# Block products of an MLP in another order, their left sums on VectorE and their first weight sums by adding transfers

## The chip, the cores and the metric

The kernel runs on one core of a Trainium2 chip. A core has five engines with a queue each: TensorE (PE) multiplies, VectorE (DVE) and ScalarE (ACT) do elementwise work, GpSimd (POOL) does elementwise work and issues transfers, and SyncE (SP) issues transfers. Each engine takes its instructions in order, and an instruction that waits holds up all that stand behind it in its queue. The metric is the device time of one execution in microseconds (us). The time before is the median of 3 runs, 786.85 us (786.6 to 787.11).

## The reference, cut to what matters

The program is one layer of a transformer in fp32 over 512 tokens of width 1024: a gated linear attention and a latent attention side by side, an output projection, and an MLP of width 4096 with a squared ReLU. The change lies in the MLP and in the turn from the output projection into it:

```python
    merged = jax.nn.sigmoid(z_ma) * y_gla + jax.nn.sigmoid(z_mb) * y_mla
    h = h + merged @ w_out[l]
    m = rmsnorm(h, g_mlp[l])
    h = h + jnp.square(jax.nn.relu(m @ w_ff1[l])) @ w_ff2[l]
return rmsnorm(h, g_final)
```

## The kernel before

**Three matmuls for one.** Each fp32 operand is split into a high part, rounded to the matmul's format (a copy on ScalarE), and a low part, the rest (a subtraction on VectorE). `mm3` (lines 87 to 90) multiplies high by high, high by low and low by high. In the profile a split's two halves are named by their tile: `f150h` and `f150l` are the high and low of the weights of phase f1, product 5, half 0.

**Seven products for eight.** The large multiplications are cut into 2 x 2 blocks, and each is done with seven block products in place of eight, for which sums of blocks are formed on either side. For the weights (the right side), with blocks B11, B12, B21, B22: product 1 takes B11, product 2 takes B21, product 5 takes B11+B12, product 6 adds B22 to that, product 4 adds B21 to that, product 3 takes B22, product 7 takes B12+B22. The sums are formed in place, in the tiles into which the blocks were loaded. So product 5's weights can be formed only after product 1's have been split. For the left side the sums are 5 = A21-A22, 6 = sum 5 - A11, 7 = A11-A21, 3 = A12 + sum 6 (the signs are the code's).

**Phases.** The hidden width of 4096 is worked through in four quarters. Each has two phases: in phase f (f0 to f3) the normed rows are multiplied by a block of `w_ff1`, in phase g (g0 to g3) its result by a block of `w_ff2`. A product of an f phase is 48 matmuls of 256 columns, a product of a g phase 24 of 512. The class `Mlp` (lines 1543 to 1682) writes a phase, the loop behind line 1859 runs through all 56 products. At each step it first calls `prepare` for the product two steps ahead: B22 is added for product 6 on VectorE (`add`, line 1577), the weights are split in two halves of 128 x 1024 (`split_right`, ACT line 1582 and DVE line 1586), and `behind` issues what may follow. There are four buffers of highs and four of lows, which is two products' worth: a product's split can begin only when the product two before it is through.

**What `behind` does, before.** After product 1's split GpSimd adds B12 to B11 (line 1577), and a transfer issued by GpSimd adds B22 from memory onto B12 (`onto`, line 1572, `accum_op`). After product 6's split such a transfer adds B21 onto B11. After 2, 3, 7 and 4 SyncE loads the blocks of the phases to come (`load`, line 1568).

**The left side in a quarter.** `keep` takes the results of an f phase's products from the accumulators into the blocks A11, A12, A21, A22 of the hidden layer, with ReLU and square, and splits those that are finished (`split_left`, through `split`, lines 93 and 94). After product 4, the last of an f phase, `left_sums` forms sum 5 on VectorE and the sums 7, 6 and 3 on GpSimd (line 1664). Their splits follow in the g phase, at its first three products. In g each product's result is added to the rows `hrow` (`add_rows`, line 1465).

**The turn into the MLP.** From the output projection on (line 1745) up to the fourth product of f0 the order of TensorE, ScalarE and VectorE is written out: `in_program_order` ties each instruction to the one before it on its engine; the same holds for GpSimd over a longer stretch. In it, rows 0 and 1 are scaled (`row_rstd` has one power on GpSimd, line 184; `scaled` is lines 1479 and 1480), transposed on TensorE (`flipped`, line 198), and turned into the left blocks of f0 with the gain: `m_upper` for rows 0 to 255 splits straight from the accumulator, `m_upper_raw` forms the unsplit blocks again on GpSimd (line 1510), `m_lower` and `m_lower_raw` do rows 256 to 511, `m_sum` forms sums (line 1539), on GpSimd unless told otherwise. Behind that stretch the order of each engine is the framework's, which goes by the program's order and by what is ready.

Of the kernel before, what the change touches and what calls it, by code (L numbers as in the profile page):

```python
# [56 lines left out]
def tile_block(ctx: ExitStack, tc: tile.TileContext, t, out: bass.AP):  # L57
# [1436 lines left out]
    def m_upper():  # L1494

        for m in (1, 2):
            m_left[m] = quarter(f"mh{m}"), quarter(f"ml{m}")
        for k in range(KD):
            hi, lo = m_left[1 + k // NP]
            src, gain = fm.block(0, k)  # L1500
            split_scaled(hi[:, k % NP], lo[:, k % NP], src, gain)

    def m_upper_raw():

        for m in (1, 2):
            hi, lo = m_left[m]
            m_raw[m] = pair_tiles(f"mr{m}")
            for b, dst in enumerate(m_raw[m]):
                c = slice(2 * b, 2 * b + 2)
                nc.gpsimd.tensor_tensor(dst, raw(hi[:, c]), raw(lo[:, c]), op=ALU.add)  # L1510

    def m_split(m):
        m_left[m] = hi, lo = quarter(f"mh{m}"), quarter(f"ml{m}")
        for b, s in enumerate(m_raw[m]):
            c = slice(2 * b, 2 * b + 2)
            split(hi[:, c], lo[:, c], s)

    def m_lower():

        a22, s1 = pair_tiles("mr4"), pair_tiles("mr5")  # L1520
        m_raw[4], m_raw[5] = a22, s1
        for b in range(2):
            for i in range(2):
                src, gain = fm.block(1, NP + 2 * b + i)
                nc.scalar.activation(a22[b][:, i], src, AF.Copy, scale=gain)
                src, gain = fm.block(1, 2 * b + i)
                nc.vector.scalar_tensor_tensor(s1[b][:, i], src, gain, a22[b][:, i], op0=ALU.mult, op1=ALU.subtract)
        m_split(5)

    def m_lower_raw():  # L1530
        m_raw[0] = a21 = pair_tiles("mr0")
        for k in range(NP):
            src, gain = fm.block(1, k)
            nc.scalar.activation(a21[k // 2][:, k % 2], src, AF.Copy, scale=gain)

    def m_sum(m, x, y, op, eng=nc.gpsimd):
        m_raw[m] = pair_tiles(f"mr{m}")
        for dst, a, b in zip(m_raw[m], m_raw[x], m_raw[y]):
            eng.tensor_tensor(dst, a, b, op=op)
# [4 lines left out]
    class Mlp:  # L1544


        def __init__(self, n):
            self.n, self.qd, self.second = n, n // 2, n % 2 == 1
            self.name = f"{'g' if self.second else 'f'}{self.qd}"
            self.order = ORDER if n == 2 * NQ - 1 else SEVEN  # L1550
# [19 lines left out]
        def onto(self, dst, x):  # L1570
            for g, d in enumerate(self.tiles(dst)):
                nc.gpsimd.dma_start(d, self.source(x, g), accum_op=ALU.add)  # L1572

        def add(self, dst, x, eng, gs=range(2)):
            for g in gs:
                a, b = self.tiles(dst)[g], self.tiles(x)[g]
                eng.tensor_tensor(a, a, b, op=ALU.add)  # L1577
# [12 lines left out]
        def behind(self, m):  # L1590

            after_ = phases[self.n + 1 : self.n + 3]
            if m == 1:
                self.add(B11, B12, nc.gpsimd)
                self.onto(B12, B22)
            elif m == 6:
                self.onto(B11, B21)
            elif m == 4:
                if len(after_) == 2:
                    after_[1].load(B11)  # L1600
            elif m in (2, 3, 7) and after_:
                after_[0].load({2: B21, 3: B22, 7: B12}[m])

        def prepare(self, m):
            if m == 6:
                self.add(B11, B22, nc.vector)
# [24 lines left out]
        def keep(self, m):  # L1631
# [16 lines left out]
            if m in (2, 3, 7):  # L1648
                self.split_left(c)

# [7 lines left out]
        def left_sums(self):  # L1658

            a11, a12, a21, a22 = (self.left[x] for x in (1, 2, 0, 4))  # L1660

            def sums(eng, dst, a, b, op):
                for d, x, y in zip(dst, a, b):
                    eng.tensor_tensor(d, x, y, op=op)  # L1664

            sums(nc.vector, a22, a21, a22, ALU.subtract)
# [264 lines left out]
```

## Time and profile before

| | us |
|---|---|
| median of 3 runs | 786.85 |
| profiled execution, its own time | 788.59 |
| its span (first to last instruction) | 786.6 |
| TensorE busy | 746.1 |
| VectorE busy | 664.6 |
| ScalarE busy | 496.3 |
| GpSimd busy | 309.3 |

The profile is of one execution. Its views are a page with each engine's busy time; a table of busy time by stretch; a list of who waited for whom; and instructions in order of time. A row in order of time has its start, its length, engine, line, operation, output<-inputs with shapes, a count if like instructions follow one another, and in brackets the idle time before it with what ended it. `x2` after a row means that the length covers two instructions. "Granted clock" is the share of TensorE's full clock: 1.00 or, in some stretches, 0.50.

### The profile page before, as it was taken

To read this page: it belongs to the slowest core of one execution; us is meant where nothing else is said; L and a number is where in the kernel's file an instruction comes from. 1 tells how busy PE (TensorE), PEld (TensorE's weight loads), DVE (VectorE), ACT (ScalarE), POOL (GpSimd) and SP (SyncE) were. 2 spreads that over 40 slices of the span, in tenths; PEclk is the share of its full clock that TensorE was granted. 3 is DMA by queue.
4 is the path that set the end of the run, shared out by engine and by line. 5 is a ranking of instruction groups with operands and counts; after the bars stand their busy time and mean duration, and the time that the engine had idled before them with its cause. 6 is when DMAs were issued, how large, how long until landed. Compare 5 with 4: busy or idle time off the path is not lost.

```text
span 786.6 us, 11492 instructions
## 1 busy us (share of the span) xinstructions
PE 746.1 (95%) x4226; PEld 650.0 (83%) x4226; DVE 664.6 (84%) x830; ACT 496.3 (63%) x807; POOL 309.3 (39%) x323
## 2 busy tenths in 40 slices
PE   9999999999999999999998698899889997999796
PEld 7888888888988988989888696799768995799575
DVE  7786887899987877988989889885998789886994
ACT  7456665768667759888565684547544674367454
POOL 0722110265457241367518326140823145140934
PEclk9999999999999999999999899999989999999898
DMA  9759580612122244587964354757546743765332
GB/s 319 229 143 255 141 202 17 108 29 67 47 74 21 72 104 120 128 226 230 204 197 107 56 162 105 212 109 195 127 87 171 174 131 80 215 150 146 53 54 107
DMA packets 78343, 105.75 MB, mean 134 GB/s; under 512 B 15792, under 2 KB 34224, under 8 KB 78288
## 3 DMA queue, kind: packets, MB, share of 16 engines
q1 hardware_dynamic: 63088, 75.64, 30.9%
q0 software_dynamic: 14912, 29.10, 21.8%
q8 instruction: 33, 0.54, 0.3%
q10 hardware_dynamic: 288, 0.28, 0.1%
q14 instruction: 22, 0.18, 0.1%
HBM read 100.03 MB, written 2.10 MB: 130 GB/s over the span
## 4 chain that ended last, share of the span: by engine, by line
PE 72%; DVE 18%; issue 6%; ACT 3%; POOL 1%; DVEq 0%; POOLq 0%; ACTq 0%
PE first L326 3%; DVE h L1465 2%; PE tp L1122 2%; DVE w L1577 2%; PE zb L88 1%; PE zb L90 1%; PE zb L89 1%; DVE f0l L94 1%; DVE f1l L94 1%; DVE f2l L94 1%; PE av L89 1%; PE av L88 1%; PE av L90 1%; DVE f3l L94 1%; PE s L88 1%
## 5 line engine op out<-in xcount | busy, mean ns | idle before, releaser
L1577 POOL TENSOR_TENSOR w<-w,w 128x1024 f32<-128x1024 f32 x15 | 41.9, 2793 | 131.2 <-DVE g010l L1586 22.3
L1572 POOL DMA_DIRECT2D w<-in_w_ff x32 | 38.8, 1224 | 59.1 <-DVE f260l L1586 10.1
L1102 DVE TENSOR_REDUCE top<-s 128x1 f32<-128x512 f32 x32 | 21.6, 682 | 4.9 <-PE s L90 4.7
L1107 ACT ACTIVATE e<-s,top 128x512 f32<-128x512 f32 x32 | 22.0, 688 | 3.5 <-DVE top L1102 2.5
L94 DVE TENSOR_TENSOR pT<-tp,pT 128x512 fp32r<-128x512 f32 x32 | 21.8, 683 | 2.4 <-ACT pT L93 1.9
L94 POOL TENSOR_TENSOR qF<-qk,qF 128x512 fp32r<-128x512 f32 x4 | 6.6, 1640 | 37.6 <-ACT qF L93 37.6
L93 ACT ACTIVATE pT<-tp 128x512 fp32r<-128x512 f32 x32 | 19.1, 596 | 3.2 <-PE tp L1122 3.2
L94 DVE TENSOR_TENSOR f2l<-f2a,f2h 128x512 fp32r<-128x512 f32 x14 | 17.7, 1276 | 3.0 <-ACT f2h L93 2.8
L94 DVE TENSOR_TENSOR f1l<-f1a,f1h 128x512 fp32r<-128x512 f32 x14 | 17.7, 1276 | 3.0 <-ACT f1h L93 2.8
L667 POOL DMA_DIRECT2D gvw<-in_w_in x4 | 4.8, 1226 | 38.7 <-DVE gvw L672 34.0
L94 DVE TENSOR_TENSOR f3l<-f3a,f3h 128x512 fp32r<-128x512 f32 x14 | 17.1, 1230 | 2.8 <-ACT f3h L93 2.8
L1122 PE MATMUL tp<-ident,e 128*128 128x128 f32 x128 | 19.4, 274 | 0.0
L88 PE MATMUL av<-pT,v 128*128 128x256 f32 x64 | 19.1, 299 | 0.0
L90 PE MATMUL av<-pT,v 128*128 128x256 f32 x64 | 18.2, 284 | 0.0
L89 PE MATMUL av<-pT,v 128*128 128x256 f32 x64 | 18.1, 283 | 0.0
L1122 PEld LDWEIGHTS tp<-ident,e 128*128 128x128 f32 x128 | 15.2, 140 | 3.2 <-ACT e L1113 0.7
L667 POOL DMA_DIRECT2D zaw<-in_w_in x4 | 4.8, 1215 | 32.7 <-DVE zaw L672 28.0
L94 DVE TENSOR_TENSOR f0l<-f0a,f0h 128x512 fp32r<-128x512 f32 x14 | 13.1, 950 | 3.7 <-ACT f0h L93 3.7
L1153 POOL TENSOR_TENSOR mx<-tb,yg 128x256 f32<-128x256 f32 x8 | 7.7, 967 | 19.8 <-DVE tb L1150 13.8
L980 POOL DMA_DIRECT2D w<-in_w_out x10 | 12.3, 1402 | 6.5 <-DVE bo60l L94 5.3
L93 ACT ACTIVATE f0h<-f0a 128x512 fp32r<-128x512 f32 x14 | 8.5, 620 | 9.2 <-POOL f0a L1664 6.8
L88 PE MATMUL s<-kbuf,q 96*128 96x512 f32 x32 | 14.1, 439 | 0.0
(2143 smaller groups left out, 3360.6 us busy)
## 6 DMA issues: line engine op xcount, KB each, us to landing
w<-in_w_ff SPq DMA_DIRECT2D x48, 512.0 KB, 4.9
w<-in_w_ff POOLq DMA_DIRECT2D x32, 512.0 KB, 6.1
w<-in_w_out POOLq DMA_DIRECT2D x10, 512.0 KB, 8.6
grw<-in_w_in SPq DMA_DIRECT2D x8, 512.0 KB, 8.6
zaw<-in_w_in SPq DMA_DIRECT2D x8, 512.0 KB, 7.0
gvw<-in_w_in SPq DMA_DIRECT2D x8, 512.0 KB, 4.5
w<-in_w_out SPq DMA_DIRECT2D x16, 256.0 KB, 5.5
w220f<-in_w_ff SPq DMA_DIRECT2D x8, 512.0 KB, 6.4
```

The costliest lines, as they stand in the source:

```text
L88: nc.tensor.matmul(acc, lh, rh, start=start, stop=False, skip_group_check=onto)
L89: nc.tensor.matmul(acc, lh, rl, start=False, stop=False, skip_group_check=onto)
L90: nc.tensor.matmul(acc, ll, rh, start=False, stop=stop, skip_group_check=onto)
L93: nc.scalar.activation(hi, src, AF.Copy)
L94: rest.tensor_tensor(lo, src, raw(hi), op=ALU.subtract)
L326: nc.tensor.matmul(f_accs[i], a[:, i * P : (i + 1) * P], b, start=k == 0 and x == 0, stop=k == KD - 1 and x == 2)
L1102: nc.vector.tensor_reduce(top, acc, axis=AX.X, op=ALU.max, negate=True)
L1107: nc.scalar.activation(e, acc, AF.Exp, bias=top, accum_out=tot[:, qt % 2 : qt % 2 + 1])
L1122: nc.tensor.transpose(tp[:, k * P : (k + 1) * P], e[:, k * P : (k + 1) * P], ident)
L1465: nc.vector.tensor_tensor(hc, hc, acc, op=op)
L1572: nc.gpsimd.dma_start(d, self.source(x, g), accum_op=ALU.add)
L1577: eng.tensor_tensor(a, a, b, op=ALU.add)
```

## The change

- The order of the products is 1, 5, 6, 7, 2, 4, 3 in place of 1, 2, 5, 6, 3, 7, 4; in f0 it is 1, 2, 5, 6, 7, 4, 3. The last phase keeps its own order 1, 5, 6, 3, 7, 4, 2.
- B11+B12 is formed by a transfer that adds B12 from memory onto B11, right behind product 1's split. B12+B22 is formed by such a transfer one phase earlier, as soon as B12 has been loaded.
- All left sums are on VectorE. Sums 5, 7 and 6 and the splits of 5, 6 and 7 stand behind product 4, sum 3 and its split behind product 3.
- At the turn into the MLP the blocks are first copied out of the accumulators with the gain and then split, so that nothing has to be formed again; the sums are on VectorE and stand next to the products that need them.

```diff
+    def m_copy(x, half, ks):
+        ...
+            nc.scalar.activation(m_raw[x][p // 2][:, p % 2], src, AF.Copy, scale=gain)
+    def m_sum(m, x, y, op, bs=range(2)):
+        ...
+            nc.vector.tensor_tensor(m_raw[m][b], m_raw[x][b], m_raw[y][b], op=op)
...
-            self.order = ORDER if n == 2 * NQ - 1 else SEVEN
+            self.order = {0: (1, 2, 5, 6, 7, 4, 3), 2 * NQ - 1: ORDER}.get(n, (1, 5, 6, 7, 2, 4, 3))
...
+        def onto(self, dst, x, gs=range(2)):
             for g in gs:
...
+                nc.gpsimd.dma_start(self.tiles(dst)[g], self.source(x, g), accum_op=ALU.add)
...
             if m == 1:
-                self.add(B11, B12, nc.gpsimd)
-                self.onto(B12, B22)
+                self.onto(B11, B12)
             elif m == 6:
                 self.onto(B11, B21)
...
             elif m in (2, 3, 7) and after_:
                 after_[0].load({2: B21, 3: B22, 7: B12}[m])
+                if m == 7:
+                    after_[0].onto(B12, B22)
...
             if m in (2, 3, 7):
                 self.split_left(c)
+            if m == 4:
+                for s in (5, 7, 6):
+                    self.left_sum(s)
+                self.split_left(6)
+                self.split_left(7)
+            elif m == 3:
+                self.left_sum(3)
+                self.split_left(3)
...
-            sums(nc.gpsimd, a21, a11, a21, ALU.subtract)
-            sums(nc.gpsimd, a11, a22, a11, ALU.subtract)
-            sums(nc.gpsimd, a12, a12, a11, ALU.add)
+        def left_sum(self, m):
+            ...
+            for d_, x_, y_ in zip(d, x, y):
+                nc.vector.tensor_tensor(d_, x_, y_, op=op)
+            self.left[m] = d
+            if m == 5:
+                low = tl([P, 2, 2, HT], F32R, "wf", 3, f"{self.name}l5")
+                self.split_left(5, [low[:, b] for b in range(2)])
...
     f0.load(B12)
     f0.load(B22)
+    f0.onto(B12, B22)
     for rb in range(2):
...
         scaled(rb, row_rstd(hparts[rb]))
...
-    m_upper()
+    for x in (1, 2):
+        m_copy(x, 0, range((x - 1) * NP, x * NP))
+        m_split(x)
     first_half_square(3, 1)
-    f0.add(B11, B12, nc.gpsimd, (0,))
+    f0.onto(B11, B12, (0,))
...
     rs3 = row_rstd(hparts[3])
+    f0.onto(B11, B12, (1,))
...
     f0.behind(2)
-    f0.add(B11, B12, nc.vector, (1,))
-    m_upper_raw()
-    f0.onto(B12, B22)
     f0.first(1, True)
...
     f0.first(2)
-    m_lower()
     f0.split_right(5, 0)
-    m_sum(6, 5, 1, ALU.subtract, nc.vector)
-    m_lower_raw()
+    for b in range(2):
+        ks = range(2 * b, 2 * b + 2)
+        m_copy(4, 1, (NP + k for k in ks))
+        m_copy(0, 1, ks)
+        m_sum(5, 0, 4, ALU.subtract, (b,))
+    m_split(5)
     f0.split_right(5, 1)
+    m_sum(6, 5, 1, ALU.subtract)
+    f0.keep(1)
     m_split(6)
-    m_sum(7, 1, 0, ALU.subtract)
-    m_sum(3, 2, 6, ALU.add)
-    f0.keep(1)
     f0.prepare(6)
     f0.first(5, True)
     f0.keep(2)
     f0.keep(5)
-    m_split(3)
-    f0.prepare(3)
+    m_sum(7, 1, 0, ALU.subtract)
+    m_split(7)
+    f0.prepare(7)
     f0.first(6)
...
-        if at < 3:
-            f_ph.split_left((6, 3, 7)[at])
```

More of the change, by code (lines that the diff above doesn't have):

```diff
@@ L1530, in m_lower_raw @@
[L1530 to L1539, printed above, removed]
+    def m_copy(x, half, ks):
+        for k in ks:
+            if x not in m_raw:
+                m_raw[x] = pair_tiles(f"mr{x}")
+            src, gain = fm.block(half, k)
+            p = k % NP
+            nc.scalar.activation(m_raw[x][p // 2][:, p % 2], src, AF.Copy, scale=gain)
```

71 lines of the change are left out of this document (20 added, 51 removed).

## The prediction

> **What bounds the kernel now.** I read the page's busy times first, then busy time by stage, then who waits for whom on TensorE, then the order of time around the worst waits.
>
> ```profile
> PE 746.1 (95%) x4226; PEld 650.0 (83%) x4226; DVE 664.6 (84%) x830; ACT 496.3 (63%) x807; POOL 309.3 (39%) x323
> ```
> TensorE is busy 95% of the span, so only its 40 us of idle time, and the half clock behind long waits, can be won. The stages of the MLP (cut where a phase's first matmul starts: f0, g0, f1, g1, f2, g2, f3, g3 up to its last product; the last row is one product of g1 alone) show where it sits. Columns: stretch and length; busy time and instructions of PE, PEld, DVE, ACT, POOL; granted clock, DMA share, GB/s.
>
> ```profile
> 412.50:469.16 56.66, 47.28 (x353) 45.42 (x352) 48.95 (x51) 38.15 (x63) 26.32 (x17) 0.94 0.46 112
> 469.16:515.79 46.63, 41.05 (x171) 32.34 (x169) 44.42 (x43) 22.14 (x28) 22.17 (x14) 0.96 0.53 135
> 515.79:556.10 40.31, 40.31 (x337) 40.31 (x336) 30.18 (x28) 28.03 (x40) 9.15 (x6) 1.00 0.65 157
> 556.10:602.82 46.72, 42.32 (x171) 32.88 (x170) 44.40 (x42) 20.11 (x25) 21.87 (x14) 0.93 0.54 135
> 602.82:643.13 40.31, 40.31 (x338) 40.31 (x336) 30.17 (x28) 28.04 (x40) 9.12 (x6) 1.00 0.66 157
> 643.13:689.84 46.71, 41.48 (x170) 31.87 (x169) 44.39 (x42) 20.10 (x25) 21.86 (x14) 0.96 0.53 135
> 689.84:730.15 40.31, 40.31 (x337) 40.30 (x336) 30.18 (x28) 27.69 (x40) 9.74 (x7) 1.00 0.60 145
> 730.15:773.82 43.67, 36.28 (x146) 28.16 (x145) 40.69 (x38) 20.69 (x32) 26.81 (x20) 0.92 0.29 48
> 591.93:597.37 5.44, 5.44 (x25) 4.50 (x24) 3.65 (x5) 2.12 (x2) 0.00 (x0) 1.00 0.79 250
> ```
> f1, f2 and f3 lose nothing: 7 products of 5.76 us. A g product takes 5.44, so seven take 38.08: g0, g1, g2 lose 8.55, 8.64, 8.63, and g3's six (32.64) lose 11.03. f0 loses 56.66 - 40.31 - 1.7 for sixteen transposes = 14.65. All that can be won in the MLP is 51.5 us. In the g stages VectorE is busy 44.4 of 46.7, and TensorE waits for it:
>
> ```profile
> PE g3z L90 <- DVE f3l L94: 4.3, 2, 3.3
> PE f0z L90 <- DVE f051l L1586: 2.5, 1, 2.5
> ```
> VectorE and GpSimd at the turn from f1 to g1:
>
> ```profile
> 551.15 1.22 DVE L1586 TENSOR_TENSOR g110l<-w,g110h 128x1024 fp32r<-128x1024 f32 x1
> 553.42 6.83 DVE L94 TENSOR_TENSOR f1l<-f1a,f1h 128x512 fp32r<-128x512 f32 x2
> 561.91 2.31 DVE L1586 TENSOR_TENSOR g121l<-w,g121h 128x1024 fp32r<-128x1024 f32 x1
> 579.75 1.21 DVE L1586 TENSOR_TENSOR g161l<-w,g161h 128x1024 fp32r<-128x1024 f32 x1
> 580.88 0.68 DVE L94 TENSOR_TENSOR f1l<-f1a,f1h 128x512 fp32r<-128x512 f32 x1
> 552.46 3.31 POOL L1577 TENSOR_TENSOR w<-w,w 128x1024 f32<-128x1024 f32 x1 [20.32 <-DVE g110l L1586]
> 561.00 6.06 POOL L1664 TENSOR_TENSOR f1a<-f1a,f1a 128x512 f32<-128x512 f32 x3
> 580.13 2.44 POOL L1572 DMA_DIRECT2D w<-in_w_ff  x2 [7.20 <-DVE g160l L1586]
> ```
> While GpSimd adds, a VectorE split of 512 columns takes 3.4 us instead of 0.68, and one of 1024 takes 2.31 instead of 1.21. While GpSimd only issues transfers (580.13) VectorE runs at full speed. Started back to back, VectorE needs 1.14 per 1024 columns (579.75 to 580.88) and 0.60 per 512.
>
> **The change, part by part.** Sums are against the profiled execution's span of 786.6 (its own time is 788.59, the median of the runs 786.85).
>
> *GpSimd's adds go, the left sums come to VectorE.* In each quarter three left sums (six instructions) move: 6 x 0.60 = 3.6 us more VectorE work, while the stretching of its other instructions ends. Count what VectorE must do from the second-to-last f product until product 6 of g can begin: lows of g's first weights 2.28; sums 5, 7, 6 and their lows, 12 x 0.60 = 7.2; lows for product 5, 2.28; keeping product 3, its lows, sum 3 and its lows, 8 x 0.60 = 4.8; adding B22 and the lows for product 6, 4.56. That is 21.1 us. Let U be the start of the last f product; the first sum can begin at U-1.4 (half of product 4's rows is out 2.9 earlier, two ScalarE passes follow), so with about 1 us of gaps the first low of product 6 is there at U+19.5. TensorE would want it at U+5.76+2x5.44 = 16.6, or 17.4 with the wait of 0.8 at product 5 (next). Wait 2.0 + 0.8 = 2.8 per g stage, where 36.85 in all was lost: 36.85 - 4 x 2.8 = **25.6 won**. Ends: 1 per stage if product 3's sums are placed behind product 6's weights, 5.5 if VectorE's order puts sums ahead of the first weights and a half clock follows. I take the counted order, as VectorE in before mostly follows the program's.
>
> *B11+B12 by an adding transfer, product 5 right behind product 1.* Before, product 2 lay between them, and f stages waited for nothing. Now the chain is: lows of product 1, transfer, high, low, product 5. Only four pairs of high and low buffers exist, so product 1's split starts as the product before it starts (U):
>
> ```profile
> 510.28 1.23 DVE L1586 TENSOR_TENSOR f110l<-w,f110h 128x1024 fp32r<-128x1024 f32 x1 [1.77 <-ACT f110h L1582]
> 512.02 3.05 DVE L1586 TENSOR_TENSOR f111l<-w,f111h 128x1024 fp32r<-128x1024 f32 x1
> L1572 POOL DMA_DIRECT2D w<-in_w_ff x2: 1204/1256/1307, 529.7 to 530.8; - x2
> DMA to landing us min/median/max: 6.1/6.8/7.5
> L1572 POOL DMA_DIRECT2D w<-in_w_ff x2: 1204/1256/1308, 580.1 to 581.3; - x2
> DMA to landing us min/median/max: 5.7/7.2/8.7
> DMA to landing us min/median/max: 5.7/6.1/10.4
> ```
> (The landings belong to the pair above each; the last line is all 32 adding transfers.) With U = 515.79 - 5.44 = 510.35 the first low is out at U+1.2, the second, unstretched, at U+2.9 (512.02+1.2). The second of a pair lands 8.6 to 9.9 after the first is issued: U+9.8 to 11.1. A high of 1.04 and a low of 1.22 follow: U+12.1 to 13.4. Product 5 needs that low at its ninth matmul of 48, U+5.44+5.76+0.96 = 12.2. Wait 0 to 1.2; I take 0.75, for f1, f2, f3: **2.3 lost**. With the longest landing, 10.4 from its own issue at U+2.9, it would be 3.3 each. In g the lows end at U+2.0 (551.15+1.22, U = 556.10 - 5.76) and U+3.2, and product 5 needs the second at U+12.8: 0.2 to 1.4, I take the 0.8 used above. The page "DMA: Bandwidth & Descriptors" of the Trainium skill (section on the anatomy of one DMA) fits a GpSimd-issued DMA as 2.0 us plus bytes over 436 GB/s, which makes an estimate of 3.2 us for 512 KB; these waits would then vanish and the sum be 5 us lower. The rows say 5.7 to 10.4, and they decide.
>
> *The other early transfer: B12+B22 of f0, ordered in GpSimd's queue ahead of the row scales.* It waits for B12's load, and GpSimd's order is written out here, so the powers (L184) that scale rows 0 and 1 queue behind it:
>
> ```profile
> 396.44 2.69 SPq L1568 DMA_DIRECT2D w<-in_w_ff  x2
> DMA to landing us min/median/max: 5.3/5.3/5.3
> 400.44 0.57 POOL L184 TENSOR_TENSOR hp<-hp,mhalf 128x1 f32<-128x1 f32 x1 [8.52 <-DVE hp L181]
> 401.04 0.72 ACT L1480 ACTIVATE ms<-h,hp 128x512 f32<-128x512 f32 x1 [0.95 <-POOL hp L184]
> 402.40 1.04 PE L198 MATMUL mb<-ident,ms 128*128 128x128 f32 x8
> 404.65 1.03 PE L198 MATMUL mb<-ident,ms 128*128 128x128 f32 x8
> ```
> The load of B12's second half is issued at 398.76 (the second of the two) and lands at 404.1; two issues of 1.2 us, the second behind that landing, keep GpSimd until 405.3. The first power moves from 400.44 to 405.3. VectorE and ScalarE, in written order too, wait with it, and so do the first transposes (402.40, scale ready at 401.8): the second group, with 0.2 of slack, moves by 4.7. TensorE has nothing else in its written order. **4.8 lost**, and a wait that long costs a stretch at half clock:
>
> ```profile
> 563.81:570.64 6.83, 4.65 (x18) 3.30 (x18) 6.73 (x6) 2.99 (x4) 5.98 (x4) 1.00 0.63 196
> 570.64:577.47 6.83, 5.62 (x13) 4.04 (x14) 6.83 (x7) 1.63 (x4) 2.21 (x2) 0.50 0.00 0
> ```
> Waits of some 2 us in the first stretch were followed by 0.50 in the second. Half of 3.4 us is **1.7 lost**. Ends: 0 if the load lands before GpSimd asks, 6.5 as summed. The page "TensorE: Matmul & The Clock Gate" (Part 1) has the clock halve only after a whole idle window of 3.4 us. By it neither this wait nor the one in f0 below need cost a half clock, and the sum would be 3.4 lower. The row above, with no such window idle, disagrees.
>
> *f0.* Now GpSimd rebuilds raw blocks and sums:
>
> ```profile
> 417.06 7.17 POOL L1510 TENSOR_TENSOR mr<-mh,ml 128x512 f32<-128x512 f32 x4
> 420.57 1.57 ACT L1525 ACTIVATE mr<-mb,gvec 128x256 f32<-128x256 f32 x4 [0.73 <-PE mb L198]
> 433.08 2.29 DVE L1586 TENSOR_TENSOR f051l<-w,f051h 128x1024 fp32r<-128x1024 f32 x1
> 441.14 1.22 DVE L1586 TENSOR_TENSOR f061l<-w,f061h 128x1024 fp32r<-128x1024 f32 x1
> 450.64 1.22 DVE L1586 TENSOR_TENSOR f031l<-w221f,f031h 128x1024 fp32r<-128x1024 f32 x1
> ```
> After, sum 6 goes behind product 5's second weights, and no add slows VectorE. Transposes done and first high made by 421.7 (1.1 later, for four more ScalarE splits), eight copies of 0.39, highs 0.52+0.52+1.04, last low 1.22: f051l ends at 428.1 instead of 435.4. The two gaps behind it stay (7.0 to the lows of product 6, 9.5 to those of the fifth product; I count 7.6 and 9.8, as the sums move in): the fifth product's second low at 445.6, its end at 450.3, with one half clock 452.0, where it now ends at 457.64. **5.6 won**. Ends 4 and 9.
>
> *At nothing:* the 1 MB more transfers in each phase (DMA share 0.53 to 0.65), and the copy in place of split at the turn, which lies beside TensorE's last output products.
>
> Sum: -25.6 + 2.3 + 4.8 + 1.7 - 5.6 = -22.4; from the median, 786.85 - 22.4 = **764.5**.
>
> **The rivals.**
> - *Slower: the second adding transfer lands late.* If it takes the 10.4 us of its own slowest row instead of 8, product 5 waits 3.3 in f and 3.2 in g, and each wait draws a half clock of 1.7. f: 3 x 5.0 - 2.3 = 12.7 more; g: 4 x 4, less 4 that product 6's wait absorbs = 12 more. 764.5 + 24.7 = **789**. It decides from landings of 10 us on, at all seven places. For it: adding transfers that shared the DMA engines with loads were the slow ones. Against: in the new order no load is issued between products 1 and 5.
> - *VectorE's order eats half the gain:* sums ahead of the first weights delay the transfer by 3 us in g: 4 x 3 = 12, **777**.
> - *The row scales don't wait* (GpSimd served in another order): -6.5, and with product 3's sums last another -7: **751**.
> - *Nothing is freed* (transfers slow VectorE like adds): g keeps its 36.85 and f pays: **790**. The row at 579.75 beside 580.13 speaks against it.
>
> **How the numbers follow.** Forecast 0.45 (own range 757 to 773), VectorE's order 0.20, no wait for the row scales 0.15, late landings 0.17, nothing freed 0.03. Faster (by over 0.2%, about what a measurement of this kernel can tell from no change) takes the first three less a little: 0.78; same 0.02; slower 0.20. The range cuts a tenth on either side: 750 to 789.
>
> **What would show it.** Splits at 0.68 and 1.22 throughout the MLP; g stages near 41; f1 to f3 near 41 with a wait for f151l and its like; L184 near 405 behind L1572, with TensorE idle some 4 us ahead of the first transposes; f0 near 50. Wrong if product 5 waits over 2 us, or if VectorE is still the last to arrive at product 6 by more than 3.

## The result, and the profile after

The changed kernel takes 794.32 us (median of 4 runs, 793.59 to 794.76), the kernel before beside it 786.98 (4 runs): a ratio of 1.0088, 95% interval 1.0071 to 1.0106. It is 0.9% slower where 2.8% faster was forecast. The page's line of busy time, and then the table of busy time by stretch, cut as for before (the turn lies ahead of the first row; f0, g0, f1, g1, f2, g2, f3, g3; columns as before):

```profile
PE 747.2 (94%) x4226; PEld 654.5 (83%) x4226; DVE 616.4 (78%) x851; ACT 501.3 (63%) x811; POOL 230.0 (29%) x292
```

```profile
418.93:468.34 49.41, 44.94 (x354) 43.69 (x352) 40.12 (x52) 38.78 (x63) 11.69 (x11) 0.97 0.66 151
468.34:518.67 50.33, 42.06 (x171) 33.86 (x169) 37.32 (x47) 21.55 (x27) 7.26 (x7) 0.90 0.65 151
518.67:559.54 40.87, 40.57 (x338) 40.37 (x336) 28.62 (x32) 28.03 (x39) 7.26 (x6) 1.00 0.74 179
559.54:607.48 47.94, 41.83 (x171) 33.70 (x169) 35.13 (x43) 20.81 (x25) 7.25 (x6) 0.93 0.65 155
607.48:648.25 40.77, 40.56 (x337) 40.36 (x336) 28.61 (x32) 28.03 (x39) 7.29 (x6) 1.00 0.74 180
648.25:696.26 48.01, 41.84 (x171) 33.71 (x169) 35.14 (x43) 20.80 (x25) 7.24 (x6) 0.93 0.66 155
696.26:737.12 40.86, 40.56 (x338) 40.36 (x336) 28.61 (x32) 28.02 (x39) 7.82 (x7) 1.00 0.71 168
737.12:779.42 42.30, 36.38 (x146) 29.16 (x145) 32.06 (x40) 22.05 (x33) 9.44 (x11) 0.92 0.26 44
```

Against the rows of before, the turn ends 6.43 us later (418.93 for 412.50), f0 is 7.25 shorter, f1 to f3 together 1.57 longer, and g0, g1 and g2 3.70, 1.22 and 1.30 longer and g3 1.37 shorter: 4.85 longer in all. With 0.3 less behind g3 the sum is +5.3, the difference of the spans (791.9 and 786.6). The medians are 7.3 apart: the execution profiled before is one of its longer ones (788.59), the one after a shorter one (793.59). VectorE's busy time in g1 did fall, from 44.40 to 35.13, and the stage grew all the same. Who waits for whom on TensorE (total, times, longest):

```profile
PE g0z L88 <- DVE f0a L1620: 5.2, 1, 5.2
PE mb L198 <- DVE ms L1479: 4.7, 1, 4.7
...
PE g1x L88 <- DVE h L1465: 3.1, 1, 3.1
...
PE g1z L88 <- DVE f1a L1620: 3.0, 1, 3.0
```

The second line is the turn. The other two kinds were in no line of the prediction. `f1a`, L1620, are the adds with which `keep` takes f1's last product (3) out of its accumulators: product 5 of g writes the same accumulators (`banks` in the code, called banks from here on). `h`, L1465, are the row adds that read product 1 of g: product 6 adds into the same accumulators. Neither is a weight. In VectorE's order of g1 they stand here:

```profile
554.42 1.22 DVE L1560 TENSOR_TENSOR g110l<-w,g110h 128x1024 fp32r<-128x1024 f32 x1
555.55 1.22 DVE L1560 TENSOR_TENSOR g111l<-w,g111h 128x1024 fp32r<-128x1024 f32 x1
...
560.30 0.68 DVE L94 TENSOR_TENSOR f1l<-f1a,f1h 128x512 fp32r<-128x512 f32 x1
562.84 1.22 DVE L1560 TENSOR_TENSOR g150l<-w,g150h 128x1024 fp32r<-128x1024 f32 x1 [1.85 <-ACT g150h L1556]
563.98 0.69 DVE L94 TENSOR_TENSOR f1l<-f1a,f1h 128x512 fp32r<-128x512 f32 x1
565.62 1.23 DVE L1560 TENSOR_TENSOR g151l<-w,g151h 128x1024 fp32r<-128x1024 f32 x1 [0.96 <-ACT g151h L1556]
566.76 0.68 DVE L94 TENSOR_TENSOR f1l<-f1a,f1h 128x512 fp32r<-128x512 f32 x1
567.37 0.68 DVE L1620 TENSOR_TENSOR f1a<-f1a,f1z 128x512 f32<-128x512 f32 x1
...
568.57 0.68 DVE L1620 TENSOR_TENSOR f1a<-f1a,f1z 128x512 f32<-128x512 f32 x1
...
573.36 1.22 DVE L1560 TENSOR_TENSOR g160l<-w,g160h 128x1024 fp32r<-128x1024 f32 x1
...
575.70 1.22 DVE L1560 TENSOR_TENSOR g161l<-w,g161h 128x1024 fp32r<-128x1024 f32 x1
...
577.75 1.28 DVE L1465 TENSOR_TENSOR h<-h,g1x 128x512 f32<-128x512 f32 x2
```

ScalarE, in front of it, waits for the two adding transfers:

```profile
561.74 1.06 ACT L1556 ACTIVATE g150h<-w 128x1024 fp32r<-128x1024 f32 x1 [2.50 <-DMA w<-in_w_ff]
562.71 0.61 ACT L93 ACTIVATE f1h<-f1a 128x512 fp32r<-128x512 f32 x1
564.53 1.06 ACT L1556 ACTIVATE g151h<-w 128x1024 fp32r<-128x1024 f32 x1 [1.21 <-DMA w<-in_w_ff]
```

U, the start of the last f product, is 559.54 - 5.76 = 553.78. The splits run at 0.68 and 1.22 as forecast. The lows of product 1, behind which the transfers are issued, are out at U+1.9 and U+3.0 (forecast 2.0 and 3.2), and the last low of product 5 at 566.85, U+13.1, also as forecast. But while ScalarE stood at `g150h` and `g151h`, the splits and adds behind them stood too, and VectorE idled 1.85 and 0.96 us. The adds that free product 5's banks run at 567.37 and 568.57, when its weights are out, and the adds that free product 6's run at 577.75.

### The profile page after: what moved, and what is told of

Same layout as the page of the kernel before. It is cut to its first block, busy times and chain, and to the rows that moved or that the text cites. A ratio compares the mean times of both kernels' runs of the same rounds, so it can differ in the third digit from the quotient of the medians.

```text
span 791.9 us, 11507 instructions
## 1 busy us (share of the span) xinstructions
PE 747.2 (94%) x4226; PEld 654.5 (83%) x4226; DVE 616.4 (78%) x851; ACT 501.3 (63%) x811; POOL 230.0 (29%) x292
## 5 line engine op out<-in xcount | busy, mean ns | idle before, releaser
L1547 POOL DMA_DIRECT2D w<-in_w_ff x48 | 58.0, 1217 | 283.4 <-DMA w<-in_w_ff 71.5
L88 PE MATMUL s<-kbuf,q 96*128 96x512 f32 x32 | 14.1, 439 | 0.0
L94 DVE TENSOR_TENSOR f0l<-f0a,f0h 128x512 fp32r<-128x512 f32 x14 | 9.4, 685 | 5.8 <-ACT f0h L93 5.8
L1153 POOL TENSOR_TENSOR mx<-tb,yg 128x256 f32<-128x256 f32 x8 | 7.7, 963 | 19.8 <-DVE tb L1150 13.8
L89 PE MATMUL s<-kbuf,q 96*128 96x512 f32 x32 | 12.6, 395 | 0.0
L90 PE MATMUL s<-kbuf,q 96*128 96x512 f32 x32 | 12.6, 393 | 0.0
L1113 ACT ACTIVATE e<-e,tot 128x512 f32<-128x512 f32 x16 | 11.6, 726 | 1.3 <-DVE tot L1112 1.3
L577 ACT ACTIVATE bds<-bd 128x512 f32<-128x512 f32 x4 | 2.4, 597 | 15.8 <-PE bd L555 15.8
L89 PEld LDWEIGHTS av<-pT,v 128*128 128x128 f32 x64 | 12.2, 190 | 0.2
```

The source lines that it names most:

```text
L88: nc.tensor.matmul(acc, lh, rh, start=start, stop=False, skip_group_check=onto)
L89: nc.tensor.matmul(acc, lh, rl, start=False, stop=False, skip_group_check=onto)
L90: nc.tensor.matmul(acc, ll, rh, start=False, stop=stop, skip_group_check=onto)
L94: rest.tensor_tensor(lo, src, raw(hi), op=ALU.subtract)
L1113: nc.scalar.activation(a, a, AF.Copy, scale=tot[:, 0:1])
L1547: nc.gpsimd.dma_start(self.tiles(dst)[g], self.source(x, g), accum_op=ALU.add)
```

## The experiments

All times are medians, and each ratio is to runs of the kernel before on the same chip (medians 787.2 to 787.7). "Order" is that of f1 to g2 and f3: new (1, 5, 6, 7, 2, 4, 3) or old (1, 2, 5, 6, 3, 7, 4). "Splits" is the place of the splits of left sums 6, 7 and 3: right behind the sums (early) or in the g stage (late). "g1" is the length of that stage, cut as above. In b2, b3 and d3 f0 and the turn are those of before.

| kernel | order | sums on | B11+B12 | splits | us | ratio, 95% interval | g1 |
|---|---|---|---|---|---|---|---|
| before | old | GpSimd | GpSimd | late | 786.98 | 1 | 46.72 |
| changed | new | VectorE | transfer | early | 794.32 | 1.0088 (1.0071 to 1.0106) | 47.94 |
| a1_turn | new | VectorE | transfer | early | 788.82 | 1.0021 (1.0011 to 1.0032) | 47.79 |
| a2_banks | new | VectorE | transfer | early | 794.44 | 1.0095 (1.0073 to 1.0116) | 48.23 |
| a3_rows | new | VectorE | transfer | early | 784.76 | 0.9974 (0.9959 to 0.9989) | 45.23 |
| a4_all | new | VectorE | transfer | early | 783.35 | 0.9954 (0.9940 to 0.9969) | 47.02 |
| b1_order | old | VectorE | transfer | early | 783.82 | 0.9956 (0.9939 to 0.9972) | 45.09 |
| b2_sums | old | VectorE | GpSimd | late | 780.08 | 0.9908 (0.9893 to 0.9922) | 44.22 |
| b3_transfer | old | GpSimd | transfer | late | 776.11 | 0.9856 (0.9838 to 0.9875) | 42.33 |
| b4_vector_add | new | VectorE | VectorE | early | 778.52 | 0.9889 (0.9872 to 0.9905) | 44.47 |
| c1_vec_banks | new | VectorE | VectorE | early | 783.82 | 0.9943 (0.9922 to 0.9964) | 47.47 |
| c2_gp_sums | old | GpSimd | transfer | late | 769.09 | 0.9766 (0.9744 to 0.9788) | 42.29 |
| c3_vec_order | old | VectorE | VectorE | early | 769.18 | 0.9763 (0.9742 to 0.9784) | 41.75 |
| d1_last_rows | old | VectorE | VectorE | early | 767.62 | 0.9751 (0.9732 to 0.9770) | 41.75 |
| d2_vec_rows | new | VectorE | VectorE | early | 780.32 | 0.9903 (0.9887 to 0.9920) | 47.47 |
| d3_both | old | VectorE | transfer | late | 773.85 | 0.9826 (0.9806 to 0.9846) | 43.32 |
| d4_gp_vec | old | GpSimd | VectorE | late | 774.28 | 0.9828 (0.9807 to 0.9849) | 42.61 |
| e1_late_order | old | VectorE | transfer | late | 765.34 | 0.9720 (0.9697 to 0.9742) | 41.04 |
| e2_late_vec | old | VectorE | VectorE | late | 762.17 | 0.9676 (0.9661 to 0.9691) | 40.82 |
| e3_late_new | new | VectorE | transfer | late | 788.96 | 1.0023 (1.0012 to 1.0035) | 46.72 |

### The turn, the banks, the row adds

The first theory was that three places in the queues account for the loss. a1_turn:

```diff
     f0.load(B22)
-    f0.onto(B12, B22)
     for rb in range(2):
         ...
         scaled(rb, row_rstd(hparts[rb]))
+    f0.onto(B12, B22)
```

> The changed kernel, with the transfer that adds B22 onto B12 of f0 moved in GpSimd's order behind the two powers that scale rows 0 and 1. Theory (the power waits only because GpSimd stands in front of it waiting for B12's load): the wait of 4.7 us ahead of the first transposes goes, and the half clock behind it (1.7), so 794.3 - 6.4 = 787.9; f0 to g3 keep their lengths. Rival (the scale is late for another reason, or the transfer now comes late for product 7 of f0): 794, with the wait moved to the fifth product of f0.

The turn's wait was rightly priced: 5.5 us less than the changed kernel, where 6.4 was expected. The stages did not all keep their lengths: in a1's profile the turn ends 7.31 us earlier, f0 is 2.51 longer and g0 0.89. The rows of the changed kernel that it undoes are GpSimd's at the turn, and VectorE's first scaling:

```profile
402.94 1.23 POOL L1547 DMA_DIRECT2D w<-in_w_ff  x1 [11.51 <-DMA w<-in_w_ff]
404.41 1.20 POOL L1547 DMA_DIRECT2D w<-in_w_ff  x1 [0.24 <-issue]
405.16 1.05 POOL L184 TENSOR_TENSOR hp<-hp,mhalf 128x1 f32<-128x1 f32 x1
```

```profile
406.24 0.49 DVE L1479 TENSOR_SCALAR ms<-h,hp 128x512 f32<-128x512 f32 x1 [6.36 <-POOL hp L184]
```

a2_banks and a3_rows move the adds that free the accumulators ahead of the weights in VectorE's order, a4_all has all three edits:

```diff
 # a2_banks: prepare(5) is called inside keep(3), behind its adds
+            if not behind and (ph.second or m != 3):
...
+            ph.keep(m, (lambda: ahead[0].prepare(ahead[1])) if m == 3 else None)
 # a3_rows: prepare(6) is called behind product 1's row adds
+        if ph.second and m == 1:
+            added = traced()
+            ahead[0].prepare(ahead[1])
+            goes_behind((added, traced()), (adding, added), SPLITTERS[1:])
```

> The changed kernel, with VectorE's two adds that take product 3's result out of its accumulators placed ahead of the split of product 5's weights of g. Theory (product 5 of g waits for the accumulators of the f phase's last product, which VectorE releases only behind weights that wait for a transfer): the waits of 5.2, 3.0, 3.1, 2.8 ahead of product 5 fall under 1, and product 6, which waits for VectorE too, takes part of it back: 1 to 3 us less per g stage, 783 to 790. Rival 1 (VectorE's load bounds the turn, whatever its order): product 6 starts when it does now, 793 to 795. Rival 2 (the adding transfer bounds product 5): the wait stays at product 5, on the low of its second half.

> The changed kernel, with VectorE's adds of product 1's result to the rows placed ahead of the add and splits for product 6 of each g stage. Theory (product 6 goes onto the accumulators that these adds must read first): the four waits of 3.1 for the rows shrink to what the weights of product 6 need, about 0.5 to 1; product 5's wait stays; 2 us per stage, 784 to 788. Rival (VectorE's load bounds): the wait turns into one for the low of product 6 and the time stays at 793 to 795.

> The changed kernel with all three: powers ahead of the transfer, product 3's adds ahead of product 5's weights, product 1's row adds ahead of product 6's weights. Theory (three queues in a wrong order, VectorE's load fits): each g stage loses about 4 to 5 instead of 10, 6.4 come back at the turn: 764 to 772. Rival (VectorE's load bounds the turn from f to g): 6.4 at the turn and 1 or 2 per stage: 780 to 786.

a2 won nothing, the time of its first rival: in g1 its wait for the banks gave place to one of 2.9 for the lows behind the transfer. a3 won 9.6, as its theory had it. a4 won 11.0, less than a1 and a3 apart (15.1): it came out at its rival's 780 to 786, not at the theory's 764 to 772. The list of waits of a4_all:

```profile
PE g0z L89 <- DVE g050l L1560: 3.5, 1, 3.5
...
PE g1z L89 <- DVE g150l L1560: 2.6, 1, 2.6
```

ScalarE in a4_all shows what is behind it:

```profile
554.44 1.06 ACT L1556 ACTIVATE g150h<-w 128x1024 fp32r<-128x1024 f32 x1 [2.70 <-DMA w<-in_w_ff]
```

So the places of the adds explain part, and behind them is the transfer.

### Each part of the change by itself

> The changed kernel with one thing put back: in f1 to g2 and in f3 the products go in the order of before (1, 2, 5, 6, 3, 7, 4); the sums stay on VectorE and B11+B12 stays an adding transfer. Theory one, the order: with product 2 between them, the transfer has 5.4 us more before product 5 asks for its lows, and the banks that product 5 wants are free a product earlier; f1 to f3 fall to 40.3 to 40.5, the g stages from 48 to 41 to 43, and the time is 765 to 775 (it still has the wait of 4.7 us at the turn). Rival, VectorE's load: the sums themselves are too much between the last f product and product 6; then the g stages stay at 46 to 48 whatever the order, and the time is 785 to 795.

> The kernel of before with one part of the change alone: the three left sums of each quarter that GpSimd does (six instructions of 128x512) are done on VectorE, in the same place of the program; GpSimd keeps adding B11+B12, and the order of the products and the turn are those of before. Theory one, contention: VectorE's splits beside those sums fall from 3.4 and 2.3 us to 0.68 and 1.22, its busy time in a g stage from 44.4 to about 38, and the g stages from 46.7 to 43 to 45: 772 to 780. Rival, VectorE's order: six more adds stand ahead of the lows that product 6 waits for, and what stretching is saved is spent again; the g stages stay at 46 to 48 and the time is 785 to 792.

> The kernel of before with another part alone: in the MLP's phases behind the turn B11+B12 is an adding transfer in place of GpSimd's two adds of 128x1024; GpSimd keeps the left sums, and the order (product 2 between 1 and 5) stays. Theory one: the transfer has product 2's time, so product 5 does not wait for it in f (f1 to f3 stay at 40.3 to 40.6), and the lows beside the two GpSimd adds are no longer stretched; 0 to 1.5 us a phase, 780 to 787. Rival, the transfer's latency: product 5 waits over 1 us in each phase, and the time is 790 to 797.

> The changed kernel with its order 1, 5, 6, 7, 2, 4, 3 kept, but from f1 on B11+B12 is added on VectorE (two adds of 128x1024, 2.3 us) right ahead of product 5's split, in place of the adding transfer; the transfer that adds B22 to B12 is issued behind product 5's split. If the latency of the transfer is what product 5 waits for in g, its wait for the lows falls from about 3 us to under 1, f1 to f3 stay within 0.6 of 40.3, each g stage is 2 to 3 us shorter and the time is 783 to 788. If it is the place of the sums in VectorE's order, or the banks, 2.3 us more of VectorE's work make it 796 to 805.

```diff
 # b1_order
-            self.order = {0: (1, 2, 5, 6, 7, 4, 3), 2 * NQ - 1: ORDER}.get(n, (1, 5, 6, 7, 2, 4, 3))
+            self.order = {0: (1, 2, 5, 6, 7, 4, 3), 2 * NQ - 1: ORDER}.get(n, SEVEN)
...
-            elif m == 3:
+            if m == self.order[-1]:
                 self.left_sum(3)
 # b2_sums, on the kernel before
-            sums(nc.gpsimd, a21, a11, a21, ALU.subtract)
+            sums(nc.vector, a21, a11, a21, ALU.subtract)
...
 # b3_transfer, on the kernel before
-                self.add(B11, B12, nc.gpsimd)
+                self.onto(B11, B12)
 # b4_vector_add
-            if m == 1:
-                self.onto(B11, B12)
+            if m == 5:
+                self.onto(B12, B22)
...
-            if m == 6:
-                self.add(B11, B22)
+            if m in (5, 6):
+                self.add(B11, B12 if m == 5 else B22)
```

In b1 sum 3 and its split have to stand behind product 4, the last of an f phase in the old order, so that edit goes with the order. Two of the parts are gains when done alone: the sums on VectorE 7.2 us (b2, at the edge of its theory's 772 to 780), the transfer 11.2 (b3, at 776.1 faster than both its ranges). b4 came out faster than both its ranges, too: it gives VectorE 2.3 us more to do in every phase and is 15.8 us faster than the changed kernel. The stages f1 and g1 of b4:

```profile
515.94:556.25 40.31, 40.31 (x337) 40.30 (x336) 28.66 (x33) 27.14 (x38) 3.77 (x4) 1.00 0.63 158
556.25:600.72 44.47, 39.50 (x170) 31.09 (x169) 38.49 (x47) 21.55 (x26) 5.93 (x5) 1.00 0.57 142
```

f1 loses nothing, and g1 keeps the full clock. The wait of 2.9 for the banks stays in b4, so it is not the transfer alone. b1 came out between its two theories, at 783.8. Its f stages are at 40.3 to 40.5, but in g1 ScalarE still stands at the transfer, and splits of left blocks are queued behind:

```profile
565.42 1.06 ACT L1556 ACTIVATE g151h<-w 128x1024 fp32r<-128x1024 f32 x1 [2.48 <-DMA w<-in_w_ff]
566.39 2.17 ACT L93 ACTIVATE f1h<-f1a 128x512 fp32r<-128x512 f32 x4
```

### VectorE's sum of work

> b4_vector_add with two more edits: at the turn the adding transfer of f0 is issued behind the two row scales (as in a1_turn), and the adds that take product 3 out of its banks stand in VectorE's order ahead of product 5's weights (as in a2_banks). In b4 product 5 waited 2.9, 2.9, 2.9 and 5.3 us for those adds. If they are late only for their place in the queue, and no transfer takes their place now, these waits go, each g stage comes to 41 to 42, and with 5.5 less at the turn the time is 757 to 765. If VectorE simply has too much work between the last f product and product 5, the wait moves to product 5's lows as it did in a2, the g stages stay at 44 to 45, and the time is 771 to 775.

> b1_order (the order of before, the adding transfer) with the turn's transfer behind the row scales, and the left sums 7, 6 and 3 of each quarter given back to GpSimd, with their splits in the g stages where before has them. Beside b1 less 5.5 for the turn (778.3) it shows what moving those sums to VectorE brings once no other add is left on GpSimd. Theory of the prediction, contention: GpSimd's sums stretch VectorE's work again and it is slower, 783 to 790. Rival, VectorE's queue: the sums ahead of product 5's and 6's weights cost more than the stretching; the g stages come to the 42.3 of b3_transfer and the time is 769 to 773.

> The corner that is missing: sums on VectorE, B11+B12 added on VectorE (as in b4_vector_add), the order of before (as in b1_order), the turn's transfer behind the row scales. b4 less 5.5 for the turn is 773.0, b1 less 5.5 is 778.3. If the new order costs something by itself (the banks of products 3 and 5), this one is 762 to 769; if the order was bad only because the transfer had no product beside it, it is 772 to 776.

c1 is b4 with the edits of a1 and a2; c3 is b1 with those of a1 and b4. c2 also takes b1 and a1, without the early splits and with this:

```diff
-                nc.vector.tensor_tensor(d_, x_, y_, op=op)
+                (nc.vector if m == 5 else nc.gpsimd).tensor_tensor(d_, x_, y_, op=op)
...
+        at = ph.order.index(m)
+        if at < 3:
+            phases[ph.n - 1].split_left((6, 3, 7)[at])
```

c1 fell outside both expectations, at 783.8: freeing the banks of product 5 earlier only made the row adds for product 6 later (4.7 us waited for `h`). c3 lies just above its first range, at 769.2. d2 then took that place away, and the sum of work showed itself:

> c1_vec_banks with the row adds of product 1 ahead of product 6's weights in all g stages (as in a3_rows). In c1 VectorE works without a gap from the start of the last f product to those row adds 22.8 us later, and product 6 waits 4.7 for them. Place in the queue: the wait goes, g stages of 42 to 43, 762 to 768. VectorE's sum of work: product 6 waits for its lows in place of the adds, 2 to 4 us, g stages of 45 to 47, 774 to 782.

> c3_vec_order with one edit in g3 alone: the row adds that take product 1 out of its banks stand in VectorE's order ahead of product 6's weights. In c3 product 6 of g3 waits 7.0 us for them, and its half clock follows. If it is their place in the queue, that wait falls to under 2, and the time is 762 to 766; if VectorE is simply that late with product 6's weights, the wait moves to g360l and the time stays at 768 to 770.

```diff
 # d2_vec_rows: c1_vec_banks and the edit of a3_rows; d1_last_rows: c3_vec_order and, in g3 alone,
+            if not behind and not (last and m == 1):
...
+        if last and m == 1:
+            added = traced()
+            ahead[0].prepare(ahead[1])
+            goes_behind((added, traced()), (adding, added), SPLITTERS[1:])
```

Busy time in d2_vec_rows from U (550.27 - 5.76 = 544.51) to the end of product 6's first weights, and product 6's first low in VectorE's order:

```profile
544.51:570.60 26.09, 20.64 (x106) 16.72 (x105) 26.06 (x34) 16.65 (x24) 4.56 (x4) 0.93 0.32 60
```

```profile
566.85 1.22 DVE L1560 TENSOR_TENSOR g160l<-w,g160h 128x1024 fp32r<-128x1024 f32 x1
```

VectorE is busy 26.06 of 26.09 us. The low is out at 568.07, U+23.6. The prediction's count gave U+19.5 for it; with the two adds of B12 that this kernel has on VectorE (2.28) and three row adds that the count left out (1.8), both put in after the run, it is U+23.6. TensorE would ask for it at U+16.6 if nothing waited before. With this order and B12's adds on VectorE, moving one thing forward made another late in c1 and in d2: d2 is at 780.3, on the side of the sum of work. d1, between its two ranges, moved the wait in g3 from 7.0 for the row adds to 4.0 for the highs of `g360`; its 1.6 us less than c3 lie within the intervals.

c2 and c3, in the old order, are both 18 us faster than the kernel before. c3 is 3.8 faster than b4 less a1's 5.5 (773.0): with B12 added on VectorE the order alone costs that much. c2 agrees with its rival, but it moves the splits of the left sums as well as the sums; e1 below parts the two.

### The parts together, and the place of the splits

> The kernel of before with both parts that were faster alone, and nothing else: left sums on VectorE (b2_sums, 7.1 less) and B11+B12 as an adding transfer (b3_transfer, 11.1 less); order and turn of before. If they add up: 767 to 770. If each had won the same thing, an end to GpSimd's adds beside VectorE's, or if the six sums stand in VectorE's queue ahead of what the transfer feeds, they do not: 778 to 786, as b1_order less its turn and f0 would have it.

> c2_gp_sums (left sums on GpSimd, order of before) with B11+B12 added on VectorE in place of the adding transfer. In c2 f1 to f3 lose 1.8 us in all to the transfer and g1 and g2 wait 1.2 each for its lows. If that latency is what is left, f1 to f3 fall to 40.3 and the time is 764 to 767; if the 2.3 us more on VectorE, stretched beside GpSimd's sums, cost more than the transfer did, it is 770 to 775.

d3 is before with the edits of b2 and b3, d4 is c2 with b4's adds. d3 is 773.9, between its two ranges: 13.8 won where the parts alone won 7.2 and 11.2, so they overlap by 4.6. d4, GpSimd's sums with B12's adds on VectorE, is 5.2 slower than c2, in its rival's range; in g1 the two are 0.3 apart, and most of the rest lies in g3, where d4's product 6 waits 8.2 us for a split of left blocks (`f3h`, ScalarE). b1 has d3's parts in d3's order, but its splits of the left sums come early; that was tried in both orders:

> b1_order with the turn's transfer behind the row scales and the splits of the left sums 6, 3 and 7 at products 1, 2 and 5 of the g stage, as in before. b1 less 5.5 for the turn is 778.3; d3_both less 5.7 for f0 is 768.2. If the early splits ahead of product 5's weights are what parts the two, 766 to 770, with g stages of 42 to 43; if it is the place of the adding transfer of B12 in GpSimd's queue ahead of the one of B11 (its second half landed 12.2 us after its issue in b1), it stays at 776 to 780.

> d1_last_rows (order of before, sums and B11+B12 on VectorE, 767.6) with the splits of the left sums 6, 3 and 7 in the g stages as in before. In d1 products 5 and 6 lose 3.6 us together in g1 and g2 and 8.0 in g3, product 6 waiting for its highs behind the late add. With the splits later the weights come earlier: g1 and g2 near 40, 762 to 766. If VectorE's sum of work sets it, only the waits change place: 766 to 770.

> The changed kernel with one part undone: the splits of the left sums 6, 7 and 3 come at products 1, 5 and 6 of the g stage, and not right behind the sums. If their place in the queues ahead of product 5's weights were the cause, products 5 and 6 of the g stages would lose 3 to 5 us less each stage: 778 to 785. If the adding transfer right behind product 1 is the cause, as b4_vector_add says, product 5 waits as before and little is won: 788 to 794.

```diff
                     self.left_sum(s)
-                self.split_left(6)
-                self.split_left(7)
...
                 self.left_sum(3)
-                self.split_left(3)
...
+        at = ph.order.index(m)
+        if at < 3:
+            phases[ph.n - 1].split_left((6, 3, 7)[at])      # (6, 7, 3) in e3_late_new
```

Stages f1 and g1 of e1_late_order, then of e2_late_vec:

```profile
505.34:545.65 40.31, 40.31 (x338) 40.31 (x336) 27.48 (x30) 28.03 (x40) 7.26 (x6) 1.00 0.75 183
545.65:586.69 41.04, 38.84 (x171) 31.38 (x169) 35.55 (x45) 19.99 (x25) 7.29 (x6) 1.00 0.73 178
```

```profile
506.54:546.86 40.32, 40.32 (x338) 40.31 (x337) 28.45 (x32) 27.39 (x39) 4.36 (x5) 1.00 0.64 157
546.86:587.68 40.82, 38.67 (x171) 31.37 (x170) 38.69 (x48) 20.80 (x26) 5.32 (x5) 1.00 0.63 155
```

In the old order the later splits win 13 us (b1 less a1's 5.5 is 778.3, e1 765.3). e2 is the fastest kernel here: 762.17, 25 us below the kernel before. e1 against c2, which differ only in the engine of the sums, says that the sums on VectorE are worth 3.8 once the rest is equal (the two intervals of the ratio just fail to touch); so it was the early splits that made b1 slow, not the sums. In the new order the later splits win 5.4: e3 has the time of its rival, but not its mechanism. Product 5 of g1 no longer waits, ScalarE still stands 3.2 and 1.6 us at the copies behind the transfers (`g150h`, `g151h`), and the wait is now product 6's, for the row adds. The list of waits of e3_late_new:

```profile
PE g1x L88 <- DVE h L1465: 4.7, 1, 4.7
```

e3 and e1 differ in the order of f1 to g2 and f3 and in the turn. 788.96 - 5.5 - 765.34 leaves **18 us for the order with the transfer in it**: the same parts give 765 with product 2 between 1 and 5, and 783 without. With early splits it is 10.5 (a1 against b1 less 5.5), and with early splits and B12 added on VectorE 3.8 (above). The corners with the left sums on VectorE, less 5.5 where a run has the turn of the changed kernel (b1, b4, e3):

| order | splits | B11+B12 by a transfer | B11+B12 added on VectorE |
|---|---|---|---|
| new | early | 788.8 (a1) | 773.0 (b4) |
| new | late | 783.5 (e3) | not run |
| old | early | 778.3 (b1) | 769.2 (c3) |
| old | late | 765.3 (e1) | 762.2 (e2, with d1's edit of g3) |

Against adds on VectorE the transfer costs 15.8 us in the new order and 9.1 in the old one, and 3.2 there with late splits. So with early splits most of the order's price, 6.7 of 10.5, is the transfer that has lost its cover; with late splits this is not shown. The 5.5 was measured on the changed kernel alone; the profiles bear it out, as g0 starts at 468.3 to 470.1 in the runs without that edit and at 462.8 to 463.8 in those with it (b2, b3 and d3, with the old turn, apart).

## Why the prediction was wrong

**What came out as summed.** The turn: 6.43 against 4.8 + 1.7, shown by a1. f0: 7.25 won against 5.6, inside its ends of 4 and 9; f0 of the changed kernel is 49.4 to 51.0 long in the profiles that have the same turn and f0, so 5.7 to 7.25 won. The f stages: 1.57 lost against 2.3, with the waits for `f151l` and its like that were forecast, 0.2 to 0.3 each. VectorE's splits at full speed (0.68 and 1.22) beside transfers: yes.

**The step that failed** is the term of 25.6, "TensorE would want it at U+5.76+2x5.44 = 16.6, or 17.4 with the wait of 0.8 at product 5 ... Wait 2.0 + 0.8 = 2.8 per g stage". g1 lost 47.94 - 38.08 = 9.86. TensorE's row for the first matmul of product 6:

```profile
578.58 0.73 PE L88 MATMUL g1x<-g160h,f1h 128*128 128x512 f32 x1 [3.08 <-DVE h L1465]
...
585.72 0.39 PE L88 MATMUL g1x<-g170h,f1h 128*128 128x512 f32 x1
```

The second row is product 7's first. Product 6 starts at U+24.8, 8.2 late instead of 2.8, and 1.7 more go in product 6 itself. Item by item, along what product 6 waited for, with what the runs showed in its place:

- The first low of product 6 was out at 574.58, U+20.8, 1.3 later than the count of 19.5. The count of work was not short (VectorE is busy 17.94 us from U to there; one add of sum 3 and two lows came behind that low instead of ahead of it), but VectorE idled 1.85 + 0.96 = 2.8 us behind the transfers. The prediction let a transfer delay the product that needs it. In the queues it delayed everything behind the copy that waits for it, on ScalarE first and then on VectorE.
- The count took product 6's weights for the last thing to arrive. It must also wait until the first row add (577.75, with 0.68 to run) has emptied product 1's bank: 578.43, 3.85 behind the low. a3, which puts the row adds first, shortens g1 by 2.7.
- Half clock: product 6 took 7.14 us (578.58 to 585.72) for 5.44, 1.7, the size that the prediction had for one. It had them in the turn and in f0, and in g in two of its alternatives (the end of 5.5 a stage and the late landings), but not in the counted 2.8.
- Product 5 waited 3.0, for banks, not 0.8 for its weights, which came when forecast. By itself this decided nothing: a2 and c1 took the wait for the banks away, and a2 was no faster, c1 slower than b4 less 5.5 (783.8 against 773.0). But product 5 drew a half clock of 1.7 as well (7.15 us, 568.19 to 575.34) and ended 3.1 to 3.2 us before product 6 began, so no more than that could be won by the row adds' place alone.

Together 2.8 + 1.3 + 3.85 + 0.15 + 1.7 = 9.8 of the 9.86. Behind the items stands what the prediction did not price: product 2 between 1 and 5 was 5.44 us of cover for the queues of ScalarE and VectorE as well as for the transfer. The prediction put the new order at 0.75 and 0.8 us of latency a phase, 5.5 in all; with the transfer in it, it measured 10 to 18 us. With the old order and late splits g1 is 41.04 (e1) and 40.82 (e2), where the prediction had 38.08 + 2.8 = 40.88. That these agree so closely is luck, as e2 has B12's adds on VectorE and waits for other tiles; but the gain from taking GpSimd's adds away was there to be had, and the order and the early splits spent it.

**The rivals.** "The second adding transfer lands late" came nearest in time (789) and not in mechanism: the two of g1 landed 5.7 and 7.4 after their issues, under the 10 at which it was to decide. "VectorE's order eats half" had the right engine, but not the mechanism: no sums delayed the transfer (the first weights' lows were out at U+1.9 and U+3.0, as forecast); what came late on VectorE stood behind the transfer. "The row scales don't wait" and "nothing is freed" fell: the wait was 4.7, and b2 shows what was freed. The text named what would make it wrong: product 5 waiting over 2 us (3.0), VectorE last at product 6 by more than 3 (3.1). Both happened.

**What stays open.** The prices overlap (a1 and a3 apart 15.1, together with a2 11.0; b2 and b3 18.4, together 13.8), so the order's price is not split further into transfer, banks and VectorE's sum of work. The new order with late splits and B12 added on VectorE was not run. Why the early splits cost 13 in the old order and 5.4 in the new is argued from the queues, not shown by itself.

## What to carry to other kernels

When work leaves one engine for another, count the receiving queue in order, from the moment the work can begin to the moment the next product may start, and count everything that product needs: its weights, and also the instructions that must empty the accumulators it writes. A product that stands between two dependent ones is cover for every queue that works between them; price its removal by what all those queues have to do in its time. An instruction that may wait for a transfer belongs behind whatever is ready without it: a1 won 5.5 us by that. a2, which did the same with two adds, won nothing, because another wait was close behind.

## What the runs showed of the hardware

- GpSimd's left sums stretch VectorE as before even with all else moved (c2_gp_sums, VectorE and GpSimd in order of time), and yet there they cost little: e1, with the sums on VectorE and the rest alike, is 3.8 us faster. With B12's adds on VectorE too they cost more: d4 against e2 is 12.1, of which e2's edit of g3 may be 1.6.

```profile
549.96 2.31 DVE L1560 TENSOR_TENSOR g121l<-w,g121h 128x1024 fp32r<-128x1024 f32 x1
...
560.43 1.21 DVE L1560 TENSOR_TENSOR g151l<-w,g151h 128x1024 fp32r<-128x1024 f32 x1
...
547.66 5.77 POOL L1645 TENSOR_TENSOR f1a<-f1a,f1a 128x512 f32<-128x512 f32 x3 [1.15 <-PE f1x L89]
```

  The Trainium skill, "SBUF — State Buffer", "Who interferes with whom", says that a VectorE instruction with two SBUF inputs contends with a GpSimd instruction that reads SBUF. The trace agrees: 2.31 us beside GpSimd's sums, 1.21 without.
- Later landings did not make a slower kernel. From issue to landing of the adding transfers in the changed kernel, and then in e1_late_order, which is 29 us faster; each time first all 48, then those issued around the start of g1 with the median (two in the changed kernel; four in e1, beside four loads):

```profile
DMA to landing us min/median/max: 5.7/6.8/11.0
w<-in_w_ff POOLq DMA_DIRECT2D x2, 512.0 KB, 6.5
```

```profile
DMA to landing us min/median/max: 5.6/8.7/12.8
w<-in_w_ff POOLq DMA_DIRECT2D x4, 512.0 KB, 9.9
```

- In the changed kernel the granted clock fell behind a wait of 3.0 us at product 5, with TensorE at work for 3.81 us of the stretch ahead:

```profile
561.68:568.51 6.83, 3.81 (x17) 2.89 (x16) 4.72 (x6) 4.11 (x6) 0.00 (x0) 0.99 0.34 62
568.51:575.34 6.83, 6.83 (x24) 5.24 (x22) 6.80 (x10) 6.63 (x10) 0.23 (x1) 0.76 0.00 1
```
